# Low parts of layer 1's weights kept in DRAM, and the chunk states as one fp32 product

## The chip, the cores and the metric

The kernel runs on one core of a Trainium2 chip. The metric is the device time of one execution in microseconds, the median of several runs. The engines are named as in the profile: PE (TensorE) multiplies matrices, DVE (VectorE), ACT (ScalarE) and POOL (GpSimd) work on elements, SP (SyncE) issues all DMA transfers here, in order, and each engine works its own queue off in order.

## The reference

One step of a two-layer decoder trunk. Layer 0 mixes tokens by causal pooling, layer 1 by a Mamba-2 scan; 1024 prompt tokens and eight sequences of eight sample tokens pass through the same weights.

```python
def pool_mixer(h, buf, start, w_in, w_mix, scale, w_out):          # layer 0
    uz = h @ w_in
    ...
    y = mixed * scale.astype(jnp.float32) * jax.nn.silu(z.astype(jnp.float32))
    return y.astype(h.dtype) @ w_out, u_ext[:, -POOL_BUF:]

def ssd_scan(x, dt, A, B, C, h0):                                  # in layer 1
    ...
    W = CB[:, :, :, None] * L * dt_t[..., None, :]
    y_diag = jnp.einsum('bcgeij,bcjgep->bcigep', W, x)
    decay_to_end = jnp.exp(a_cum_t[..., -1:] - a_cum_t) * dt_t
    chunk_states = jnp.einsum('bcjgn,bcgej,bcjgep->bcgepn', B, decay_to_end, x)

def ssd_mixer(h, conv_buf, ssm_state, w_in, ...):                  # layer 1
    proj = h @ w_in                  # z, x, B, C and the time steps
    ...                              # convolution, ssd_scan, gate, norm
    return y.astype(h.dtype) @ w_out, new_conv, new_ssm.astype(ssm_state.dtype)
```

The model width is 1024, the inner width 2048; there are four groups of eight heads of 64, a state of 128, and chunks of 128 tokens. All is fp32.

## The kernel before

The tokens go through in two passes h = 0, 1 of 544 columns (512 of the prompt, 32 of the samples), features on the partitions: layer 0 for both passes, then layer 1 for both. The last output products of a layer's pass (`finish`, `pending`) run inside the next pass.

A product is made in fp32r. Each operand is cut into a high part, its fp32r rounding, and a low part, the rest; `product` (L125) adds hi x hi, hi x lo and lo x hi in PSUM, per half of the tokens (272 columns) and per 128 rows of the weight. So a weight unit of 128 x 1024 numbers (512 KB) is 48 matmuls of 272 columns, in two halves for an input unit and four for an output unit. `unit` (L110) loads it into `raw` (two buffers), ACT casts it to `whi` (L119), and DVE or POOL makes `wlo` = `raw` - `whi` (L122; three buffers each). Layer 0 has 112 units. Layer 1 has 57: 40 of `w_sin`, 16 of `w_sout`, and the small `w_dt`; both of its passes make all of them anew, and the last output group loads two a second time. The switch `lowv` gives every L122 to DVE in layer 0 and in the last group, and alternates DVE and POOL otherwise. PSUM has three `big` buffers for products.

In layer 1, a group has six convolved tiles (four of x, then B and C), four gates z and four output units. `ssd_common` (L553) turns B into token-major tiles `bt`, chunk by chunk, through the PSUM tile `tr` (two buffers); `bt` has a high and a low part, and the low part is a DVE subtract (L565) that reads `tr`. `ssd` (L579) goes over the four chunks for a quad of heads: POOL masks the decays `bA`, ACT takes four exponentials (L596), DVE multiplies (L597) and scales x (`xd`, `xs`, L604), and PE makes the diagonal part and the chunk state. For the state `xs` is cut in two by ACT and POOL:

```python
xe = sp.tile([P, 2, 2 * P], F32R, name="xe")
S.copy(xe[:, 0], xs)
G.tensor_tensor(out=xe[:, 1], in0=xs, in1=xe[:, 0], op=ALU.subtract)
for a, (w, k) in enumerate(((0, 0), (0, 1), (1, 0))):
    PE.matmul(pst, bt[:, w], xe[:, k], start=a == 0, stop=a == 2)
```

There are 64 such products (4 groups, 2 quads, 4 chunks, 2 passes).

The order on each engine is set by a scheduler at build time: it takes the instructions in the order of the code, those under `high_priority` (a unit's load, cast and subtract, and the evacuation of products) first, and puts others where its own plan has an engine free.

Of the kernel before, what the change touches and what calls it, by code (L numbers as in the profile page):

```python
# [16 lines left out]
P = 128  # L17
# [25 lines left out]
# columns of the constants array  # L43
# [6 lines left out]
# columns of the parameters array  # L50
# [26 lines left out]
def pool_ssd_step(ctx, tc, xin, spool, sconv, sssm, w_pin, w_mix, w_pout, w_sin, w_dt, w_sout, params, consts,  # L77
# [26 lines left out]
    lowv = [2, 0]  # L104
# [4 lines left out]
    # ---------------------------------------------------------------- helpers  # L109
    def unit(src, cols=1024):  # L110
        raw = wp.tile([P, 1024], F32, name="raw")
        with tc.high_priority():
            return unit1(raw, src, cols)

    def unit1(raw, src, cols):
# [4 lines left out]
        eng = V if lowv[0] and lowv[1] % lowv[0] == 0 else G  # L120
        lowv[1] += 1
        eng.tensor_tensor(out=lo[:, :cols], in0=raw[:, :cols], in1=hi[:, :cols], op=ALU.subtract)  # L122
        return hi, lo

    def product(m, hi, lo, act, kts, width, off, evac, halves=(0, 1)):  # L125
        """evac(n, sum over kt of (hi+lo)[:, kt, off:off+m]^T (ah+al)[kt]) for the halves n of the tokens"""
# [16 lines left out]
    def to_stream(dst, halo, step, r=None):  # L143
        """puts a product (times r) behind the halos of the prompt and of the sample sequences"""
# [39 lines left out]
    def spread(pr, r, quarters):  # L184
        """quarters of r side by side, on every partition"""
# [4 lines left out]
    def rsqrt(ps, count, out=None):  # L190
        """rsqrt(sums / count + eps), on every partition"""
# [30 lines left out]
    def normed(src, r, layer):  # L222
        """hi and lo parts of RMSNorm(x), features on the partitions"""
# [23 lines left out]
    def project(src, act, u, evac):  # L247
        hi, lo = unit(src[u])
# [17 lines left out]
    def out_units(src, g, y, sink):  # L266
        for dpair in range(4):
            out_unit(unit(src[g * 4 + dpair]), dpair, y, sink)

    # ---------------------------------------------------------------- layer 0  # L270
    def layer0(h, act, pending, nxt):
# [48 lines left out]
        def begin():  # L320
            """the first two products, as x comes in; 1 / rms follows them"""
            us = [u_open(m, sp.tile([P, 2 * T], F32, name="ys", bufs=2)[:, :UW]) for m in range(2)]
            lowv[0] = 1
# [36 lines left out]
            lowv[0] = 1  # L360
# [12 lines left out]
        def mix_part(g, p, z):  # L373
            tiles = []
            for mp in range(2):
                hi, lo = unit(w_mix[g * 2 + mp])
                for tt in range(2):
# [51 lines left out]
    # ---------------------------------------------------------------- layer 1  # L429
# [9 lines left out]
    def dt_part(h, act):  # L439
        """time steps and decays; (chunk or sequence, head) on the partitions, their tokens in the columns"""  # L440
        hi, lo = unit(w_dt, KT * NH)
# [18 lines left out]
        # softplus: max(v, 0) + log1p(exp(-|v|)), log1p(e) = 2 artanh(e / (2 + e))  # L460
# [24 lines left out]
        # decay of a whole chunk or sequence, on every partition  # L485
# [7 lines left out]
        # token-major copies  # L493
# [22 lines left out]
    def conv_part(h, act, g, j):  # L516
# [25 lines left out]
        # silu(2 a) = a (1 + tanh a)  # L542
# [10 lines left out]
    def ssd_common(B, C):  # L553
        """per chunk: B with the tokens on the partitions, and the products of B and C"""
        out = []
        for c in range(NCH):
# [432 lines left out]
```

## Time and profile before

| | |
|---|---|
| time, median of 3 runs | 1641.78 us (1641.44 to 1650.25) |
| span of the profiled execution | 1636.0 us, so 5.8 us below the median of the runs |
| PE busy | 1574.1 us (96%) |
| DVE busy | 1173.2 us (72%) |
| ACT busy | 693.1 us (42%) |
| POOL busy | 571.1 us (35%) |
| moved by DMA | 196.75 MB, 120 GB/s on average |

The profile shows one execution; the profiled execution's own time is known as its span, from its first instruction to its last. Layer 0 fills the span up to about 690 us, layer 1 the rest, and its second pass begins at about 1130 us; from about 1590 us on comes the tail, in which the last outputs are normed. Busy shares are means over all of it, so the stages have to be read one by one. A wait is put down to the instruction that ended it.

### The profile page before, as it was taken

What the parts mean: (1) busy time and instruction counts of PE and PEld (TensorE: products, weight loads), DVE (VectorE), ACT (ScalarE), POOL (GpSimd) and SP (SyncE); (2) the same over time, 40 slices, a digit from 0 to 9 for tenths busy, and PEclk for the clock granted to TensorE, in tenths of its full rate; (3) what the DMA queues carried; (4) which work ended last, traced back from release to release, by engine and by line L of the source; (5) the groups of instructions that cost most, each with busy time, mean ns of one, the idle gap of its engine ahead of it and who ended that gap; (6) DMA issues with size and microseconds to landing.
All of it is one profiled execution on the core that took longest, in us unless ns stands there. A gap on an engine that the chain in (4) does not pass through costs nothing. (4 is left out here: it accounts for less than half of the span.)

```text
span 1636.0 us, 32593 instructions
## 1 busy us (share of the span) xinstructions
PE 1574.1 (96%) x12708; PEld 1520.0 (93%) x12708; DVE 1173.2 (72%) x2086; ACT 693.1 (42%) x1405; POOL 571.1 (35%) x657
## 2 busy tenths in 40 slices
PE   9999999999999999989999999999898799899996
PEld 8999999999999999989999999988887799889985
DVE  6566576753646465777885877888869967968877
ACT  5431313333323333455555545544544455435432
POOL 1200000021110010267545455444648546654523
PEclk9999999999999999999999999999999999999998
DMA  5523333345322334336334254344444345353431
GB/s 188 153 91 92 91 99 113 116 134 162 100 87 91 97 99 129 92 114 190 111 126 135 87 150 137 116 132 118 128 130 127 122 126 139 104 148 98 153 118 68
DMA packets 114154, 196.75 MB, mean 120 GB/s; under 512 B 27600, under 2 KB 65616, under 8 KB 114000
## 3 DMA queue, kind: packets, MB, share of 16 engines
q1 hardware_dynamic: 114000, 194.67, 39.5%
q8 instruction: 100, 1.64, 0.4%
q14 instruction: 54, 0.44, 0.1%
HBM read 172.94 MB, written 21.67 MB: 119 GB/s over the span
## 5 line engine op out<-in xcount | busy, mean ns | idle before, releaser
L135 PE MATMUL big<-ah,whi 128*128 128x272 f32 (+1 forms) x2304 | 670.1, 291 | 5.4 <-ACT u L147 5.4
L135 PE MATMUL big<-al,whi 128*128 128x272 f32 (+1 forms) x2304 | 669.1, 290 | 0.0
L135 PE MATMUL big<-ah,wlo 128*128 128x272 f32 (+1 forms) x2304 | 668.7, 290 | 0.0
L135 PEld LDWEIGHTS big<-ah,whi 128*128 128x128 f32 (+1 forms) x2304 | 435.3, 189 | 8.7 <-ACT u L147 5.8
L135 PEld LDWEIGHTS big<-ah,wlo 128*128 128x128 f32 (+1 forms) x2304 | 435.7, 189 | 1.7 <-issue 0.9
L135 PEld LDWEIGHTS big<-al,whi 128*128 128x128 f32 (+1 forms) x2304 | 435.4, 189 | 1.8 <-issue 1.3
L135 PE MATMUL big<-y,whi 128*128 128x272 f32 x2048 | 402.8, 292 | 7.6 <-DVE X L748 6.0
L119 ACT CAST whi<-raw 128x1024 fp32r<-128x1024 f32 (+1 forms) x228 | 237.5, 1041 | 339.2 <-PE big L135 321.6
L135 PEld LDWEIGHTS big<-y,whi 128*128 128x128 f32 x2048 | 323.8, 189 | 14.1 <-DVE X L748 8.0
L122 DVE TENSOR_TENSOR wlo<-raw,whi 128x1024 fp32r<-128x1024 f32 (+1 forms) x171 | 215.4, 1260 | 133.3 <-ACT whi L119 131.3
L135 PE MATMUL big<-y,wlo 128*128 128x272 f32 x1024 | 297.7, 291 | 0.0
L135 PEld LDWEIGHTS big<-y,wlo 128*128 128x128 f32 x1024 | 194.0, 189 | 1.2 <-issue 1.1
L122 POOL TENSOR_TENSOR wlo<-raw,whi 128x1024 fp32r<-128x1024 f32 (+1 forms) x57 | 139.7, 2451 | 99.1 <-ACT whi L119 99.1
L532 DVE SCALAR_TENSOR_TENSOR win<-u,par,win 128x556 f32<-128x556 f32 x144 | 142.6, 990 | 14.1 <-ACT win L530 7.9
L291 POOL COPY uc<-u 128x15 f32<-128x15 f32 x30 | 20.1, 671 | 247.6 <-ACT u L147 167.9
L596 ACT ACTIVATE L<-bA,nat 128x128 f32<-128x128 f32 x256 | 82.3, 392 | 54.8 <-PE dg L607 39.5
L135 PE MATMUL big<-p,whi 128*128 128x272 f32 x512 | 96.4, 288 | 0.0
L389 DVE TENSOR_TENSOR X<-X,big 128x272 f32<-128x272 f32 x128 | 55.0, 432 | 55.2 <-PE big L135 55.2
L698 POOL TENSOR_TENSOR ho<-hs,cdb 128x256 f32<-128x256 f32 x64 | 57.4, 899 | 99.0 <-DMA out_ssm_s_dram<-ho 51.6
L592 POOL TENSOR_SCALAR_AFFINE_SELECT bA<-bA 128x512 f32<-128x512 f32 x64 | 53.4, 835 | 102.7 <-DMA bA<-acd 94.5
L135 PEld LDWEIGHTS big<-p,whi 128*128 128x128 f32 x512 | 80.2, 188 | 0.0
L135 PE MATMUL big<-p,wlo 128*128 128x272 f32 x256 | 73.6, 288 | 0.0
(214 smaller groups left out, 2115.4 us busy)
## 6 DMA issues: line engine op xcount, KB each, us to landing
raw<-in_w_sin_dram SPq DMA_DIRECT2D x80, 512.0 KB, 3.7
raw<-in_w_pin_dram SPq DMA_DIRECT2D x64, 512.0 KB, 3.6
raw<-in_w_sout_dram SPq DMA_DIRECT2D x34, 512.0 KB, 3.6
raw<-in_w_pout_dram SPq DMA_DIRECT2D x32, 512.0 KB, 3.6
bA<-acd SPq DMA_DIRECT2D x64, 256.0 KB, 3.8
hs<-in_sssm_dram SPq DMA_DIRECT2D x64, 128.0 KB, 2.8
raw<-in_w_mix_dram SPq DMA_DIRECT2D x16, 512.0 KB, 3.6
out_ssm_s_dram<-ho SPq DMA_DIRECT2D x64, 128.0 KB, 2.1
```

The source lines that it names most:

```text
L119: S.copy(hi[:, :cols], raw[:, :cols])
L122: eng.tensor_tensor(out=lo[:, :cols], in0=raw[:, :cols], in1=hi[:, :cols], op=ALU.subtract)
L135: PE.matmul(ps, w[:, wsl], x[:, cols], start=first, stop=kt == kts - 1 and a == 2)
L291: G.tensor_copy(out=uc[:, m], in_=u[:, LP:LP + HALO])
L389: return lambda n, ps: V.tensor_tensor(out=half(X[d], n), in0=half(X[d], n), in1=ps, op=ALU.add)
L532: V.scalar_tensor_tensor(out=a[:, :n], in0=x[:, k:k + n], scalar=pcol(V_CW + ti * 4 + k), in1=a[:, :n], op0=ALU.mult, op1=ALU.add)
L592: G.affine_select(out=bA, in_=bA, pattern=[[0, 4], [1, Q]], compare_op=ALU.is_ge, fill=-1e30, base=0, channel_multiplier=-1)
L596: S.activation(out=L[:, e], in_=bA[:, e], func=AF.Exp, bias=nat[:, 0, ci + e:ci + e + 1])
L698: G.tensor_tensor(out=heads(ho), in0=heads(hs), in1=by_head(cdb, (NCH + b) * NH + h0), op=ALU.mult)
```

## The change

Three things are done. `later` and `stash` go through layer 1's weights in 113 pieces, 112 of 512 columns and one of 256: a load into an `L` buffer (three), a cast on ACT into a `bA` buffer (two), a subtract on DVE, and a store into `low`, 57 tensors in DRAM. One piece is asked for with each unit of layer 0, the rest before layer 1. `unit` takes the number of such a tensor: then `wlo` is loaded from it and not computed; without one the subtract is always DVE's. And the chunk state is one fp32 product of `bt` and `xs` without parts, with two buffers for `xs` where there was one.

```diff
+    def stash(n):
+        for k, src, a, b in todo[:n]:
+            raw = sp.tile([P, 512], F32, name="L", bufs=3)[:, :b - a]
+            nc.sync.dma_start(out=raw, in_=src[:, a:b])
+            hl = sp.tile([P, 512], F32R, name="bA", bufs=2)[:, :b - a]
+            S.copy(hl, raw)
+            V.tensor_tensor(out=hl, in0=raw, in1=hl, op=ALU.subtract)
+            nc.sync.dma_start(out=low[k][:, a:b], in_=hl.bitcast(F32))
+        del todo[:n]
...
         S.copy(hi[:, :cols], raw[:, :cols])
-        eng = V if lowv[0] and lowv[1] % lowv[0] == 0 else G
-        lowv[1] += 1
-        eng.tensor_tensor(out=lo[:, :cols], in0=raw[:, :cols], in1=hi[:, :cols], op=ALU.subtract)
+        if k is None:
+            V.tensor_tensor(out=lo[:, :cols], in0=raw[:, :cols], in1=hi[:, :cols], op=ALU.subtract)
+        else:
+            nc.sync.dma_start(out=lo[:, :cols].bitcast(F32), in_=low[k][:, :cols])
         return hi, lo
...
     def project(src, act, u, evac):
-        hi, lo = unit(src[u])
+        hi, lo = unit(src[u], k=LOW_IN + u if src is w_sin else None)
+        stash(1)
         product(P, hi, lo, act, KT, P, 0, evac)
...
-            bt = sp.tile([P, 2, NS], F32R, name="bt", bufs=NCH)
-            S.copy(bt[:, 0], pb[:, 0])
-            V.tensor_tensor(out=bt[:, 1], in0=pb[:, 0], in1=bt[:, 0], op=ALU.subtract)
+            bt = sp.tile([P, NS], F32, name="bt", bufs=NCH)
+            S.copy(bt, pb[:, 0])
...
-            xe = sp.tile([P, 2, 2 * P], F32R, name="xe")
-            S.copy(xe[:, 0], xs)
-            G.tensor_tensor(out=xe[:, 1], in0=xs, in1=xe[:, 0], op=ALU.subtract)
-            for a, (w, k) in enumerate(((0, 0), (0, 1), (1, 0))):
-                PE.matmul(pst, bt[:, w], xe[:, k], start=a == 0, stop=a == 2)
+            PE.matmul(pst, bt, xs, start=True, stop=True)
...
+    later()
     fin, act = layer0(0, None, None, second)
...
     fin, act = layer0(1, act, fin, lambda: normed(x2d[0], rstd[0], 1))
-    lowv[0] = 2
+    stash(len(todo))
     started = head(0, act)
```

The scheduler's order moves with it. On SP in the first pass of layer 0, from the gates of the second pooling group to its next inputs (`raw` is a weight unit, `u` a tile's old tokens), there stood before:

```order
L282 DMA u_1516<-in_spool_dram 128x92
L290 DMA out_pool_s_dram<-u_1060 128x92
L116 DMA raw_1395<-in_w_pin_dram 128x1024
L116 DMA raw_1456<-in_w_pin_dram 128x1024
L116 DMA raw_1519<-in_w_pin_dram 128x1024
L282 DMA u_1594<-in_spool_dram 128x92
L116 DMA raw_1597<-in_w_pin_dram 128x1024
```

In the changed kernel the same place reads so (L133 loads a piece, L137 stores a low part, L146 loads a unit):

```order
L133 DMA L_2633<-in_w_sout_dram 128x512
L316 DMA u_1669<-in_spool_dram 128x92
L146 DMA raw_1603<-in_w_pin_dram 128x1024
L137 DMA low21_107<-bA_2501 128x512
L133 DMA L_2702<-in_w_sout_dram 128x512
L137 DMA low21_107<-bA_2568 128x512
L133 DMA L_2788<-in_w_sout_dram 128x512
L146 DMA raw_1672<-in_w_pin_dram 128x1024
```

Between two units there are now two loads and two stores of pieces. It is so from the third unit of the kernel on to the 58th, almost everywhere; by then all 113 pieces are done.

On DVE in the second pass of layer 1, where the second group begins (L820 scales the first pass's outputs, L719 makes a gate), there stood before:

```order
L820 SCALAR_TENSOR_TENSOR X7_10593<-X7_10593,par_76,rr_15316 128x544
L532 SCALAR_TENSOR_TENSOR win1_16208<-u_16144,par_76,win1_16208 128x556
L597 TENSOR_TENSOR L_15839<-L_15839,bs_15787 128x512
L565 TENSOR_TENSOR bt_15789<-tr_15784,bt_15789 128x128
L719 SCALAR_TENSOR_TENSOR z0_16456<-z0_16456,big_16490 128x272
L597 TENSOR_TENSOR L_15880<-L_15880,bs_15795 128x512
L565 TENSOR_TENSOR bt_15797<-tr_15792,bt_15797 128x128
```

Now (L848 is the old L820, L629 the old L597, L565 the old L532, a step of the convolution):

```order
L848 SCALAR_TENSOR_TENSOR X7_11240<-X7_11240,par_76,rr_15831 128x544
L578 SCALAR_TENSOR_TENSOR p2_16207<-u_16138,win0_16202 128x512
L582 SCALAR_TENSOR_TENSOR p2_16207<-u_16138,win0_16202 128x32
L649 TENSOR_TENSOR ys_16342<-of_16371,bE_16368 128x2x128
L629 TENSOR_TENSOR L_16350<-L_16350,bs_16302 128x512
L629 TENSOR_TENSOR L_16386<-L_16386,bs_16309 128x512
L565 SCALAR_TENSOR_TENSOR win1_16275<-u_16211,par_76,win1_16275 128x556
L629 TENSOR_TENSOR L_16422<-L_16422,bs_16316 128x512
L678 TENSOR_SCALAR Bm_16333<-tr_16331,cst_75 96x128 x4
```

The two subtracts that read `tr` are gone from between the others, and what frees `tr` is a copy on ACT.

On POOL, in the third group of the first pass (L632 decays a state, L592 masks `bA`), there stood before:

```order
L632 TENSOR_TENSOR hf0_11185<-hf0_11145,cdb_7758 128x256
L625 TENSOR_TENSOR xe_11179<-xs_11162,xe_11179 128x256
L592 AFFINE_SELECT bA_11563<-bA_11563 128x512
L625 TENSOR_TENSOR xe_11220<-xs_11203,xe_11220 128x256
L632 TENSOR_TENSOR hf0_11226<-hf0_11185,cdb_7758 128x256
L122 TENSOR_TENSOR wlo_11967<-raw_11964,whi_11966 128x1024
L632 TENSOR_TENSOR hf0_11267<-hf0_11226,cdb_7758 128x256
L625 TENSOR_TENSOR xe_11261<-xs_11244,xe_11261 128x256
```

Now (L660 and L624 are the old L632 and L592):

```order
L660 TENSOR_TENSOR hf0_11818<-hf0_11783,cdb_8493 128x256
L624 AFFINE_SELECT bA_12140<-bA_12140 128x512
L624 AFFINE_SELECT bA_12176<-bA_12176 128x512
L660 TENSOR_TENSOR hf0_11854<-hf0_11818,cdb_8493 128x256
L553 MEMSET u_12902 128x3
L557 COPY u_12902<-cin_8385 128x4x3
L660 TENSOR_TENSOR hf0_11890<-hf0_11854,cdb_8493 128x256
L624 AFFINE_SELECT bA_12212<-bA_12212 128x512
```

The subtracts of `xe` and of the weight unit are gone, and the masks and states follow each other.

## Rows read from the trace of the kernel before

**Rows 1.** Stages: length, busy PE, PEld, DVE, ACT, POOL; clock; DMA share, GB/s.

```profile
0.00:350.00 350.00, 346.44 (x2782) 343.01 (x2782) 224.51 (x401) 121.10 (x176) 26.27 (x54) 1.00 0.38 116
350.00:690.00 340.00, 340.00 (x2718) 338.90 (x2717) 191.60 (x302) 118.82 (x196) 41.12 (x44) 1.00 0.37 110
...
870.00:1050.00 180.00, 176.17 (x1452) 168.79 (x1451) 140.27 (x253) 90.43 (x211) 93.82 (x113) 1.00 0.41 123
...
1230.00:1410.00 180.00, 159.67 (x1244) 153.02 (x1243) 151.09 (x231) 88.88 (x197) 112.76 (x114) 0.95 0.41 124
...
690.00:1590.00 900.00, 856.90 (x6955) 810.25 (x6954) 720.66 (x1315) 442.51 (x1011) 488.59 (x544) 0.99 0.43 128
```

**Rows 2.** PE's waits from 690 us: releaser, us in total, times, longest.

```profile
PE tr L559 <- DVE bt L565: 11.7, 7, 2.7
PE stt L696 <- DVE ho L699: 8.6, 6, 4.3
PE big L135 <- DVE X L748: 6.0, 5, 3.5
PE big L135 <- ACT u L147: 5.4, 2, 2.8
PE tr L168 <- POOL ssq L214: 3.1, 1, 3.1
```

**Rows 3.** Stretches of half clock in layer 1, the longest of five, and their sum.

```profile
1250.20:1257.00 6.80, 5.51 (x24) 5.51 (x25) 6.80 (x6) 3.52 (x7) 6.80 (x8) 0.50 0.37 116
...
sum 20.00, PE 18.34 PEld 18.06 DVE 16.97 ACT 10.03 POOL 10.94; mean PE 3.67 PEld 3.61 DVE 3.39 ACT 2.01 POOL 2.19
```

**Rows 4.** Chain that ended last, in order of time: start, us, matmuls.

```profile
901.44 17.66 PE big L135 x142
...
1621.27 3.73 PE stt L845 x16
```

**Rows 5.** Timeline of PE: the three products of a chunk state, and what follows.

```profile
974.82 0.51 PE L627 MATMUL stt<-xe,bt 128*128 128x256 f32 x3
975.16 0.42 PE L135 MATMUL big<-y,whi 128*128 128x272 f32 x2
```

**Rows 6.** DVE from 690 us by line: busy us, mean ns; idle before.

```profile
L532 DVE SCALAR_TENSOR_TENSOR win<-u,par,win 128x556 f32<-128x556 f32 x141 | 140.2, 994 | 14.1 <-ACT win L530 7.9 <-ACT sat L512 4.2
L122 DVE TENSOR_TENSOR wlo<-raw,whi 128x1024 fp32r<-128x1024 f32 x60 | 79.8, 1331 | 14.4 <-ACT whi L119 12.6 <-POOL cd L507 0.6
L597 DVE TENSOR_TENSOR L<-L,bs 128x512 f32<-128x512 f32 x64 | 61.6, 962 | 5.1 <-ACT bs L562 3.0 <-ACT L L596 2.0
```

**Rows 7.** Two of these lines alone: duration ns min/median/max, first and last start.

```profile
L532 DVE SCALAR_TENSOR_TENSOR win<-u,par,win x141: 775/798/4040, 690.5 to 1523.4; 128x556 f32<-128x556 f32 x141
L597 DVE TENSOR_TENSOR L<-L,bs x64: 669/684/2906, 707.8 to 1554.9; 128x512 f32<-128x512 f32 x64
```

**Rows 8.** Timelines of DVE and of POOL at one moment: start, us.

```profile
1398.46 2.88 DVE L597 TENSOR_TENSOR L<-L,bs 128x512 f32<-128x512 f32 x1
...
1397.87 2.92 POOL L122 TENSOR_TENSOR wlo<-raw,whi 128x1024 fp32r<-128x1024 f32 x1
```

**Rows 9.** POOL from 690 us by line.

```profile
L122 POOL TENSOR_TENSOR wlo<-raw,whi 128x1024 fp32r<-128x1024 f32 (+1 forms) x54 | 132.5, 2454 | 40.0 <-ACT whi L119 40.0
...
L625 POOL TENSOR_TENSOR xe<-xs,xe 128x256 fp32r<-128x256 f32 x64 | 54.5, 851 | 31.2 <-ACT xe L624 31.2
```

**Rows 10.** An ACT cast of 544 columns: duration ns min/median/max.

```profile
L240 ACT CAST p<-sq x32: 630/647/652, 34.6 to 609.5; 128x544 fp32r<-128x544 f32 x32
```

**Rows 11.** DMA issues: count, KB each, median us to landing.

```profile
raw<-in_w_sin_dram SPq DMA_DIRECT2D x80, 512.0 KB, 3.7
...
x2d<-X SPq DMA_DIRECT2D x16, 272.0 KB, 4.1
```

**Rows 12.** Timeline of SP: one issue.

```profile
32.82 0.33 SPq L290 DMA_DIRECT2D out_pool_s_dram<-u  x1
```

**Rows 13.** The stretch of most DMA traffic at the start, columns as in rows 1.

```profile
9.00:12.00 3.00, 2.27 (x26) 1.70 (x27) 2.74 (x3) 3.00 (x5) 1.74 (x2) 1.00 1.03 397
```

More of the change, by code (lines that the diff above doesn't have):

```diff
@@ L103, in pool_ssd_step, with later, inputs, unit @@
     rstd = [None, None]
-    lowv = [2, 0]
     def pcol(i):
         return par[:, i:i + 1]
-    def unit(src, cols=1024):
+    LOW_IN, LOW_OUT, LOW_DT = 0, 40, 56
+    low = [dp.tile([P, 1024], F32, name=f"low{i}") for i in range(57)]
+    todo = []
+    def later():
+        def inputs(g, js):
+            return [16 + (g * 4 + j if j < 4 else 16 + (j - 4) * 4 + g) for j in js]
+        order = [(LOW_DT, w_dt)] + [(LOW_IN + u, w_sin[u]) for u in inputs(0, (4, 5, 0, 1))]
+        for g in range(NG):
+            us = inputs(g, (2, 3)) + [g * 4 + t for t in range(4)]
+            if g + 1 < NG:
+                us += inputs(g + 1, (4, 5, 0, 1))
+            order += [(LOW_IN + u, w_sin[u]) for u in us]
+            order += [(LOW_OUT + g * 4 + d, w_sout[g * 4 + d]) for d in range(4)]
+        for k, src in order:
+            n = KT * NH if k == LOW_DT else 1024
+            for c in range(0, n, 512):
+                todo.append((k, src, c, min(c + 512, n)))
+    def stash(n):
[7 more added lines that the diff above has]
+        del todo[:n]
+    def unit(src, cols=1024, k=None):
         raw = wp.tile([P, 1024], F32, name="raw")
         with tc.high_priority():
-            return unit1(raw, src, cols)
-    def unit1(raw, src, cols):
+            return unit1(raw, src, cols, k)
+    def unit1(raw, src, cols, k=None):
         nc.sync.dma_start(out=raw[:, :cols], in_=src)
@@ L267, in out_units @@
         for dpair in range(4):
-            out_unit(unit(src[g * 4 + dpair]), dpair, y, sink)
+            w = unit(src[g * 4 + dpair], k=LOW_OUT + g * 4 + dpair if src is w_sout else None)
+            stash(1)
+            out_unit(w, dpair, y, sink)
     def layer0(h, act, pending, nxt):
@@ L322, in begin @@
             us = [u_open(m, sp.tile([P, 2 * T], F32, name="ys", bufs=2)[:, :UW]) for m in range(2)]
-            lowv[0] = 1
             pss = [[big.tile([P, 512], F32, name="big") for n in range(2)],
@@ L359, in begin @@
             nc.sync.dma_start(out=cst, in_=consts)
-            lowv[0] = 1
             with tc.high_priority():
@@ L376, in mix_part @@
                 hi, lo = unit(w_mix[g * 2 + mp])
+                stash(1)
                 for tt in range(2):
@@ L439, in dt_part @@
     def dt_part(h, act):
-        hi, lo = unit(w_dt, KT * NH)
+        hi, lo = unit(w_dt, KT * NH, LOW_DT)
         dts = sp.tile([P, 5, TQ], F32, name="dts")
@@ L601, in ssd @@
             xd = sp.tile([P, 2 * P], F32, name="xd", bufs=2)
-            xs = sp.tile([P, 2 * P], F32, name="xs")
+            xs = sp.tile([P, 2 * P], F32, name="xs", bufs=2)
             for k, x1 in enumerate((xd, xs)):
@@ L674, in ssd_sample @@
         xd = sp.tile([P, 2 * P], F32, name="xd", bufs=2)
-        xs = sp.tile([P, 2 * P], F32, name="xs")
+        xs = sp.tile([P, 2 * P], F32, name="xs", bufs=2)
         V.tensor_tensor(out=heads(xd[:SM]), in0=heads(px[:SM]), in1=by_head(sat[:SM, 1], h0), op=ALU.mult)
@@ L869, in finish_last @@
             src = w_sout[(NG - 1) * 4:]
+            lows = LOW_OUT + (NG - 1) * 4
             w = []
-            lowv[0] = 1
             for dpair in range(4):
-                w.append(unit(src[dpair]))
+                w.append(unit(src[dpair], k=lows + dpair))
                 out_unit(w[dpair], dpair, y, add, (0,))
@@ L877, in finish_last @@
             close(0, range(KT))
-            out_unit(unit(src[1]), 1, y, add, (1,))
+            out_unit(unit(src[1], k=lows + 1), 1, y, add, (1,))
             close(1, (6, 7, 4, 5, 0, 1))
             r0 = norm(0, range(KT), False)
-            out_unit(unit(src[0]), 0, y, sink, (1,))
+            out_unit(unit(src[0], k=lows), 0, y, sink, (1,))
             close(1, (2, 3))
@@ L897, in second @@
         return normed(xin[1], rstd[1], 0)
+    later()
     fin, act = layer0(0, None, None, second)
     S.copy(idr, ident)
-    lowv[0] = 1
     fin, act = layer0(1, act, fin, lambda: normed(x2d[0], rstd[0], 1))
-    lowv[0] = 2
+    stash(len(todo))
     started = head(0, act)
```

## The prediction, made before the changed kernel ran

> **What bounds the kernel now.** I read the stages first, then who made TensorE wait, then what the engine it waited for was doing. Columns in the stage table are length, busy time of PE, PE's weight loads, DVE, ACT and POOL, granted clock, DMA share, GB/s. In layer 0 PE is the bound without a break: 340.00 of 340 us busy in the second half, 346.44 of 350 in the first, where the rest is the start [rows 1]. Nothing that relieves another engine there can bring time. In layer 1 up to the tail PE is busy 856.90 of 900 us: 43.1 us are idle [rows 1]. The waits [rows 2] name DVE for most: the transposes of B wait for the subtract L565 that frees their PSUM buffer (11.7 us), state products for the add L699 (8.6), output products for L748 (6.0). Others hang on ACT and POOL (5.4, 3.1). Idleness has a second price: in layer 1 there are five stretches, 20.0 us together, at a granted clock of 0.50, that is 1.2 instead of 2.4 GHz, each just behind such a gap [rows 3]; they cost half their length, 10 us. So some 53 us are to be won in layer 1, and no more.
>
> How idle time follows DVE's load is read in the same table: with DVE busy 140.27 of 180 us (78%) PE idles 3.8 us, with 151.09 (84%) 20.3, with 224.51 of 350 (64%) or 191.60 of 340 only at the start or not at all.
>
> **The change part by part.** The sum is made against the profiled span, 1636.0 us; the median of the runs, 1641.78, is 5.8 us above, and I add the terms to the median.
>
> *The product on PE.* Per chunk three fp32r products of 256 columns become one fp32 product; the starts show 0.34 us from the first of the three to the next matmul [rows 5]. The nearest fp32 row with 128 x 128 weights: eight products of 272 columns, two instructions each, took 3.73 us, 0.466 each, so 0.44 for 256 [rows 4]. That is 0.10 us more, 64 times: **+6 us**, all on the bound engine. Bounds: 0, and +14 if each also loses a slot of a plain matmul (17.66 us / 142 = 0.124 us [rows 4]).
>
> *What leaves DVE and POOL in layer 1.* DVE had 60 weight subtracts there, 79.8 us [rows 6]; the last four units of layer 0's output weights keep theirs, so some 74 us leave, and the 32 subtracts L565 too. POOL loses 132.5 us of weight subtracts and 54.5 us of L625 [rows 9], and ACT the cast before it. With POOL's subtracts something else goes: DVE's L532 has a median of 798 ns and a mean of 994, L597 684 and 962 [rows 6, 7], which over 141 and 64 instructions is 27.6 + 17.8 = 45 us of stretching. A long one stands exactly beside a weight subtract of POOL: L597 for 2.88 us from 1398.46, POOL's from 1397.87 for 2.92 [rows 8]. Other POOL work may stretch them too, and other DVE lines are stretched that I don't count; I take 45. DVE in 690 to 1590 then falls from 720.66 by some 70 (the others lie in the tail) and 45 to about 605 us, 67%.
> The Trainium skill (SBUF — State Buffer, section "SBUF: two separate sides") says that the port which VectorE shares with GpSimd is an exclusive lock held for the whole instruction. The row of 2.88 us agrees. By that rule every stretch beside these two POOL operations would go, in lines not counted here too; that is the third rival's way.
>
> *What that is worth.* At 67% the stages above say less than 3.8 us of idleness per 180; I take 2.8, so 14 us of the 43 stay: **-29 us**. By cause: the waits for L565 become waits for an ACT copy that is there already, L625 is gone, L699 and L748 find a shorter queue; what stays is the start of a pass (time steps, norms), where chains and not loads decide. Bounds: -43, and 0 if each wait finds another last arrival. Of the slow clock's 10 us I take **-7**, as it follows the gaps. In the tail DVE loses a few subtracts of 1.3 us [rows 6], while the last norm's chain stays: **-1** (0 to -4).
>
> *The stash in layer 0.* 112 pieces of 512 columns and one of 256: a load, a cast on ACT, a subtract on DVE, a store. The order does not spread them over layer 0: it puts two into each weight unit for the first 58 units, and none later. A unit is 48 matmuls, 6.0 us at 0.124. A cast is about 0.62 us (0.647 for 544 columns [rows 10]), a subtract 0.68 (as L597's median). DVE gets 113 x 0.68 = 77 us in the first 350, from 64% to 86%; ACT 70, to 55%. What hides it is the depth in front of PE: three weight buffers and three PSUM buffers, two units and two half products ahead. The 86% is the level at which layer 1 loses 20 us in 180, but there the stretches were part of it, and in layer 0 POOL is busy only 26.27 of 350 us [rows 1]. **+4 us**; bounds 0 and +40 (20.3 x 350 / 180, were it like layer 1).
>
> *The loads in layer 1.* Each unit loads its low part, 512 KB more, into a buffer that PE has just left, so SP waits for PE where it waited for the subtract, and the scan's own loads queue behind. A load of that size lands after 3.7 us [rows 11]; the low part is needed two units, 12 us, after its buffer is free. So the weights are hidden with 8 us to spare; the scan's loads may come a little late: **+2 us** (0 to +8).
>
> Sum: +6 - 29 - 7 - 1 + 4 + 2 = -25, so 1611 for the span and **1617 us**.
>
> **The rivals.**
> *The waits change hands.* The gaps stay, with another engine at their end: ACT stands in order behind a weight cast that itself waits for PE, SP behind a low load, and the copies of B or the scan's loads come as late as DVE did. For it: B's chain runs through ACT, and the gaps at the start of a pass are chains. Against: the ordered queue of ACT loses the cast L624 and has 442.51 busy of 900 us [rows 1]. If 33 of 43 us stay and 8 of 10 at the slow clock: +6 - 10 - 2 + 4 + 2 = 0: **1642 us**.
> *The stash's own loop sets layer 0's pace (slower).* It has two buffers and the order ties two pieces to a unit. A buffer comes round after cast 0.62, subtract 0.68, issue 0.33 [rows 12], and the store's landing: 4.1 us for 272 KB [rows 11], 5.7 together, against a unit's 6.0. The next unit's weight cast stands behind it in ACT's queue. If landing takes 5.1 us in the crowd, a unit takes 6.7 and 58 units lose 41 us less the 12 us of lead: +29, which against -29 elsewhere is even; at 5.4 it is 1.0 us a unit, +46, and **1659 us**. So it decides from a mean landing of 5.1 us. For it: loads and stores come to 262 GB/s from weights and pieces, about 290 with the rest of the first stage's traffic. Against: the queue moved 397 GB/s in 9 to 12 us [rows 13], and ACT, at 55%, has 2.7 us of a unit free before the next weight cast.
> The Trainium skill (DMA: Bandwidth & Descriptors, section "Specifications") gives about 358 GB/s as one core's share of HBM; the row of 397 GB/s stands above it, and by either the traffic fits, so it does not raise this chance.
> *Nearly all idleness goes.* DVE relieved of more stretching than counted, 4 us stay, 1 at the slow clock: +6 - 39 - 9 - 2 + 0 + 0 = -44: **1598 us**.
> *It does not do what it says:* low parts land after PE wants them. Excluded by the 8 us above but for a jam of the queue; 2 in 100, counted as slower.
>
> **How the numbers follow.** Forecast 1606 to 1631: 0.46. Nearly all goes, 1593 to 1606: 0.20. Waits change hands, 1631 to 1650: 0.19. The loop, over 1650: 0.13, and the last 0.02. The range 1598 to 1649 leaves out the better half of the third rival's cases (0.06 to 0.1) and the slower ones (0.12). Half a per cent, 8 us, is about what a measurement tells from no change: below 1633.6 faster, 0.66; to 1650 same, 0.19; above, slower, 0.15.
>
> **What would show it.** Right: in layer 1 PE idles 10 to 20 us in the 900, no wait for the B subtract or L625 is left, the medians and means of L532 and L597 fall together, DVE is near 67%, the state product shows two instructions of about 0.22 us apart, at most two stretches at 0.50 clock remain; layer 0 still shows no gap over a microsecond behind the start, and DVE some 86% in its first half. Wrong: gaps in the first 350 us behind ACT casts that wait for a store (the loop), or gaps in layer 1 of the old size that end with ACT or a DMA (changed hands).

## The result, and the profile after

The changed kernel takes **1614.78 us** (median of four runs, 1614.12 to 1620.24), the kernel before 1641.61 in the same comparison; the ratio is 0.984, with a 95% interval of 0.982 to 0.986. The profiled span fell from 1636.0 to 1612.3 us. The forecast was 1617 us, faster. So the size is right. The reason, as the runs below show, is so only in part.

I read the stages first. Columns as in [rows 1]: the stretch, its length, busy time of PE, PE's weight loads, DVE, ACT and POOL, clock, DMA share, GB/s. Kernel after:

```profile
0.00:350.00 350.00, 338.76 (x2689) 333.60 (x2690) 282.57 (x499) 179.30 (x276) 28.25 (x50) 0.99 0.85 276
350.00:690.00 340.00, 340.00 (x2718) 338.90 (x2717) 187.92 (x296) 119.24 (x194) 30.33 (x40) 1.00 0.41 122
690.00:1570.00 880.00, 865.05 (x6992) 818.01 (x6991) 586.51 (x1254) 433.12 (x965) 253.36 (x430) 0.99 0.62 197
690.00:1590.00 900.00, 883.36 (x7168) 835.86 (x7168) 602.21 (x1284) 437.38 (x972) 266.33 (x445) 0.99 0.61 195
```

In layer 1 PE idles 880 - 865.05 = 15.0 us, where 43.1 of 900 stood before [rows 1]; DVE is at 67%. In the first 350 us PE has 2689 matmuls behind it, before it was 2782: 93 fewer, at 0.124 us [rows 4] 11.6 us. The second half of layer 0 is as gapless as it was. So layer 1 gave and layer 0 took.

What PE waits for in layer 1 (releaser, us in total, times, longest), kernel after:

```profile
PE big L166 <- DVE X L776: 3.5, 3, 2.5
PE big L166 <- DVE z L747: 3.3, 2, 2.8
PE tr L219 <- DVE dts L212: 2.4, 2, 1.6
PE stt L724 <- DVE ho L727: 2.3, 3, 1.2
...
PE tr L592 <- ACT bt L597: 0.5, 1, 0.5
```

Against [rows 2]: the 11.7 us for the second part of `bt` became 0.5 us for ACT's copy; the 8.6 us for `ho` (then L699, now L727) became 2.3, the 6.0 for X (then L748, now L776) 3.5. What is left are mostly chains at the start of a pass (`dts`, X, z).

Stretches at half the clock (0.50 is 1.2 of 2.4 GHz), kernel after, the first in layer 0, two in layer 1:

```profile
87.00:93.80 6.80, 4.99 (x27) 4.51 (x28) 6.77 (x18) 3.45 (x5) 1.13 (x4) 0.50 0.75 248
1087.10:1093.90 6.80, 6.03 (x28) 5.45 (x29) 6.80 (x14) 3.76 (x9) 0.61 (x1) 0.50 0.41 131
1230.40:1233.80 3.40, 3.40 (x17) 3.40 (x16) 3.40 (x4) 0.00 (x0) 3.15 (x3) 0.51 0.99 314
```

Layer 1 has 10.2 us of them, before 20.0 [rows 3]. Each stands again behind a gap of PE: 2.8 us that end at 1087.9, 2.5 at 1230.0, and in layer 0 4.9 at 87.4.

That gap in layer 0, on the timelines of PE and then of ACT (start, us; in brackets the idle time ahead and who ended it):

```profile
82.25 0.28 PE L166 MATMUL big<-ah,wlo 128*128 128x272 f32 x1
87.42 0.68 PE L199 MATMUL tr<-ssq,ones 128*32 128x136 f32 x8 [4.89 <-POOL ssq L245]
...
80.80 0.63 ACT L135 CAST bA<-L 128x512 fp32r<-128x512 f32 x1
81.33 1.05 ACT L149 CAST whi<-raw 128x1024 fp32r<-128x1024 f32 x1
85.23 0.66 ACT L244 ACTIVATE sq<-sq 128x544 f32<-128x544 f32 x1 [2.86 <-DMA sq<-in_xin_dram]
```

PE wants the column sums of the second pass's x. The load of the last tile of x stands on SP between the loads and stores of the pieces; it goes out at 80.35 and lands at 85.1. Then come ACT's square, POOL's add, and PE. The chain of waits of the same stretch shows the pieces themselves (start, us, what):

```profile
42.83 6.41 DMA low<-bA
56.25 4.86 DMA low<-bA
62.55 4.42 DMA low<-bA
67.72 4.31 DMA low<-bA
73.50 5.21 DMA low<-bA
80.35 4.78 DMA sq<-in_xin_dram
```

Last, the operations the prediction spoke of. DVE's two stretched lines in layer 1 (busy us, mean ns | idle before):

```profile
L565 DVE SCALAR_TENSOR_TENSOR win<-u,par,win 128x556 f32<-128x556 f32 x144 | 118.4, 823 | 46.6 <-ACT win L563 43.9
L629 DVE TENSOR_TENSOR L<-L,bs 128x512 f32<-128x512 f32 x64 | 50.2, 796 | 8.7 <-ACT L L628 4.9 <-ACT bs L595 3.7
```

The means were 994 and 962 ns [rows 6]: they fell together. And the state product (duration ns min/median/max, first and last start):

```profile
L655 PE MATMUL stt<-xs,bt x128: 377/379/483, 728.5 to 1546.7; 128*128 128x256 f32 x128
```

It is two instructions, 128 for 64 products.

### The profile page after: what moved, and what is told of

Same layout as the page of the kernel before. It is cut to its first block, busy times and chain, and to the rows that moved or that the text cites. A ratio compares the mean times of both kernels' runs of the same rounds, so it can differ in the third digit from the quotient of the medians.

```text
span 1612.3 us, 33214 instructions
## 1 busy us (share of the span) xinstructions
PE 1571.3 (97%) x12644; PEld 1515.7 (94%) x12644; DVE 1086.4 (67%) x2108; ACT 740.6 (46%) x1454; POOL 325.7 (20%) x536
## 4 chain that ended last, share of the span: by engine, by line
PE 81%; DMA 8%; DVE 5%; ACT 2%; issue 2%; POOL 1%; SPq 0%; DVEq 0%; ACTq 0%; POOLq 0%
PE big L166 70%; DMA low<-bA 4%; PE dg L639 2%; PE stt L655 2%; PE of L648 2%; DMA bA<-acd 1%; DMA bAs<-asd 1%; PE tr L632 1%; DMA sq<-x2d 1%; DVE bA L136 1%; DMA L<-in_w_sin_dram 1%; PE big L386 1%; PE stt L724 1%; PE of L720 1%; DVE wlo L151 1%
## 5 line engine op out<-in xcount | busy, mean ns | idle before, releaser
L151 DVE TENSOR_TENSOR wlo<-raw,whi 128x1024 fp32r<-128x1024 f32 x112 | 139.2, 1243 | 107.6 <-ACT whi L149 105.7
L565 DVE SCALAR_TENSOR_TENSOR win<-u,par,win 128x556 f32<-128x556 f32 x144 | 118.4, 823 | 46.6 <-ACT win L563 43.9
L135 ACT CAST bA<-L 128x512 fp32r<-128x512 f32 (+1 forms) x113 | 69.9, 619 | 95.4 <-DMA low<-bA 80.0
L136 DVE TENSOR_TENSOR bA<-L,bA 128x512 fp32r<-128x512 f32 (+1 forms) x113 | 78.9, 701 | 32.9 <-ACT bA L135 32.7
L624 POOL TENSOR_SCALAR_AFFINE_SELECT bA<-bA 128x512 f32<-128x512 f32 x64 | 48.5, 759 | 162.6 <-DMA bA<-acd 136.0
L726 POOL TENSOR_TENSOR ho<-hs,cdb 128x256 f32<-128x256 f32 x64 | 49.4, 778 | 138.4 <-DMA out_ssm_s_dram<-ho 79.5
L178 ACT COPY u<-big 128x272 f32<-128x272 f32 (+2 forms) x192 | 52.6, 308 | 50.9 <-PE big L166 34.4
```

Source lines behind the costliest of these rows:

```text
L135: S.copy(hl, raw)
L136: V.tensor_tensor(out=hl, in0=raw, in1=hl, op=ALU.subtract)
L151: V.tensor_tensor(out=lo[:, :cols], in0=raw[:, :cols], in1=hi[:, :cols], op=ALU.subtract)
L178: S.copy(out, ps)
L565: V.scalar_tensor_tensor(out=a[:, :n], in0=x[:, k:k + n], scalar=pcol(V_CW + ti * 4 + k), in1=a[:, :n], op0=ALU.mult, op1=ALU.add)
L624: G.affine_select(out=bA, in_=bA, pattern=[[0, 4], [1, Q]], compare_op=ALU.is_ge, fill=-1e30, base=0, channel_multiplier=-1)
```

## The experiments

All times are medians; "layer 0" is when the first step of the scan's convolution (the line that reads `win<-u,par,win`) starts, "layer 1" the time from its first start to its last, in the profiled execution; the last two columns are DVE's busy time and PE's idle time in 690 to 1590 us (in the faster kernels a little of the tail is in it).

| kernel | us | ratio to before (95%) | layer 0 | layer 1 | DVE | PE idle |
|---|---|---|---|---|---|---|
| before | 1641.6 | | 683.0 | 840.4 | 720.66 | 43.1 |
| after | 1614.8 | 0.984 (0.982 to 0.986) | 693.5 | 810.6 | 602.21 | 16.6 |
| product alone | 1634.7 | 0.996 (0.994 to 0.997) | 683.0 | 842.9 | 703.77 | 36.3 |
| low parts from DRAM alone | 1625.6 | 0.989 (0.987 to 0.992) | 696.9 | 818.4 | 602.22 | 26.2 |
| all subtracts on DVE | 1625.9 | 0.989 (0.984 to 0.994) | 683.3 | 827.9 | 721.85 | 34.0 |
| after, POOL's load put back | 1640.6 | 0.999 (0.997 to 1.001) | 695.9 | 831.0 | 622.42 | 29.4 |
| after, no pieces | 1597.8 | 0.973 (0.971 to 0.975) | 681.6 | 803.7 | 603.40 | 22.9 |
| after, pieces spread | 1605.3 | 0.977 (0.975 to 0.980) | 690.6 | 803.2 | 604.03 | 14.2 |
| all subtracts on DVE, and product | 1602.4 | 0.975 (0.974 to 0.977) | 681.9 | 810.0 | 719.64 | 16.5 |
| that, and the squares' adds on DVE | 1596.3 | 0.973 (0.971 to 0.975) | 683.4 | 802.2 | 739.97 | 19.8 |

The kernel without pieces and the last one reach the tail earlier; from 690 to 1570 us they idle 14.8 and 14.0 us, as the changed kernel does with 15.0.

**The two halves apart.** The product alone, on the kernel before:

```diff
-            bt = sp.tile([P, 2, NS], F32R, name="bt", bufs=NCH)
-            S.copy(bt[:, 0], pb[:, 0])
-            V.tensor_tensor(out=bt[:, 1], in0=pb[:, 0], in1=bt[:, 0], op=ALU.subtract)
+            bt = sp.tile([P, NS], F32, name="bt", bufs=NCH)
+            S.copy(bt, pb[:, 0])
...
+            PE.matmul(pst, bt, xs, start=True, stop=True)
```

> The kernel before with the state product of the change alone: one plain fp32 product of the chunk's B and x, no second part of B, no cast and no POOL subtract of x; the weights' low parts are still made in layer 1, on VectorE and GpSimd in turn. My theory, that the gain is VectorE's queue getting shorter and no longer stretched beside the weight subtracts, leaves 60 weight subtracts and most of the stretching here: the waits for the B subtract (11.7 us) go, the product costs 64 x 0.08 = 5 us more, some 6 us of other idleness goes with GpSimd's subtract of x: about 1629 us, L532 at a mean of 900 to 1000 ns still. The rival, that the waits for B's subtract and the product's three parts were the cause, gives the whole gain without layer 0's stash: 1641.6 - 26.8 - 11.7, about 1603. A second rival, that the waits change hands, gives 1642 to 1647 (the product's 5 us and nothing back).

And the changed kernel with these lines as they were before:

> The changed kernel with the state product of the kernel before (three fp32r products, B's second part by a VectorE subtract out of PSUM, x's by GpSimd); the low parts still come from DRAM. My theory gives most of the gain to this half: layer 0 11.7 us longer as in the changed kernel, layer 1 with 5 us less of PE for the products and some 10 us of idleness more than the changed kernel (B's subtract), so 1614.8 + 5 = about 1620; L532's mean near 850 ns. If the product's half were the cause: 1641.6 + 11.7 = 1653. If the two halves only add up, this one and the product alone together give -26.8.

They gave -7 and -16 us, together -23 of the -27. The rival that the waits for B's subtract were the cause falls (1603 expected, 1634.7 measured). Both ended between 5 and 6 us above what I expected.

**Load or stretching.** In the kernel before, all of layer 1's weight subtracts go to DVE:

```diff
-    lowv[0] = 2
+    lowv[0] = 1
     started = head(0, act)
```

> The kernel before with all weight subtracts of layer 1 on VectorE and none on GpSimd (in before they take turns). It sets VectorE's load against the stretching. VectorE gets some 54 subtracts of 1.24 us more (+67 us on the 720 of 690 to 1590 us) and, by the theory that GpSimd's weight subtracts stretched L532 and L597, loses up to 45 us of stretching: about 745 us, 83%, so the idleness of layer 1 stays near 43 us: about 1641. If the load alone decides and nothing is stretched less: 88% and some 20 us more, 1660. If the stretching (or GpSimd's 2.9 us subtract in the chain of a unit) alone decides: 43 down to 20 us, 1615 to 1620. The means of L532 and L597 say which: 994 and 962 ns, or 820 and 790.

1625.9 us. The stage row of this kernel:

```profile
690.00:1590.00 900.00, 866.02 (x7050) 823.16 (x7049) 721.85 (x1382) 444.26 (x1015) 376.05 (x488) 0.98 0.44 129
```

DVE's lines in 690 to 1570 us:

```profile
L122 DVE TENSOR_TENSOR wlo<-raw,whi 128x1024 fp32r<-128x1024 f32 x110 | 145.5, 1323 | 22.0 <-ACT whi L119 19.5 <-PE dg L607 0.9
L532 DVE SCALAR_TENSOR_TENSOR win<-u,par,win 128x556 f32<-128x556 f32 x141 | 122.1, 866 | 3.5 <-ACT win L530 0.6 <-POOL cc L527 0.5 <-POOL bA L592 0.3
L597 DVE TENSOR_TENSOR L<-L,bs 128x512 f32<-128x512 f32 x64 | 50.0, 781 | 1.2 <-ACT L L596 1.2
```

And PE's largest wait in 690 to 1590 us:

```profile
PE big L135 <- ACT u L147: 12.9, 3, 8.9
```

DVE does 113 weight subtracts in 690 to 1590 us where it did 57, 150.4 us against 76.0, and its busy time is 721.85 us against 720.66. What 56 subtracts add, the lines that are less stretched give back: 18.1 us in L532, 11.6 in L597, and 29.6 in four lines that the forecast did not count (L244, L549, L665, L753). With the same load PE idles 9 us less, and 8.9 us of the rest is a single wait.

The opposite edit: the changed kernel, with POOL's subtracts back, off the path:

```diff
             nc.sync.dma_start(out=lo[:, :cols].bitcast(F32), in_=low[k][:, :cols])
+            turn[0] += 1
+            if turn[0] % 2 == 0:
+                for a in range(0, cols, 512):
+                    b = min(a + 512, cols)
+                    G.tensor_tensor(out=dump[:, :b - a], in0=raw[:, a:b], in1=hi[:, a:b], op=ALU.subtract)
```

> The changed kernel with GpSimd's load put back off the path: in every second unit of layer 1 GpSimd subtracts the weights' high part from the weights as in the kernel before, in two pieces of 512 columns, into a tile that nobody reads. The low parts still come from DRAM. By the theory that these subtracts stretch VectorE, L565's mean goes from 823 back towards 990 ns and L629's from 796 to 960, VectorE gets up to 45 us more in layer 1 (67 to 72%), and the idleness of 15 us grows by 4 to 12: 1619 to 1627. By the rival that only VectorE's own subtracts and the chain through them counted: 1614.8, the means unchanged. Buffers of weights come free later by GpSimd's reading of them, which may cost a little in either case.

1640.6 us: the whole gain is gone, and the loss is more than twice what I expected. The stage row:

```profile
690.00:1590.00 900.00, 870.61 (x6989) 820.48 (x6988) 622.42 (x1254) 428.30 (x964) 408.63 (x538) 0.99 0.61 192
```

The lines of POOL's subtract and of DVE's two in 690 to 1570 us:

```profile
L161 POOL TENSOR_TENSOR dump<-raw,whi 128x512 f32<-128x512 f32 x106 | 150.0, 1415 | 38.8 <-ACT whi L152 37.6
L573 DVE SCALAR_TENSOR_TENSOR win<-u,par,win 128x556 f32<-128x556 f32 x144 | 134.8, 936 | 41.2 <-ACT win L571 36.6 <-ACT sat L553 2.1
L637 DVE TENSOR_TENSOR L<-L,bs 128x512 f32<-128x512 f32 x64 | 52.4, 827 | 9.9 <-ACT L L636 5.1 <-ACT bs L603 4.4
```

And one moment on the timelines of DVE and of POOL:

```profile
1407.99 2.68 DVE L573 SCALAR_TENSOR_TENSOR win<-u,par,win 128x556 f32<-128x556 f32 x2
...
1408.79 1.28 POOL L161 TENSOR_TENSOR dump<-raw,whi 128x512 f32<-128x512 f32 x1
```

Nobody reads `dump`. At 1408 two steps of the convolution, 1.6 us at their median of 798 ns, take 2.68 us, with POOL's subtract of 1.28 us beside the second. L573's mean went back from 823 to 936 ns, but L637's only from 796 to 827, where I had expected 960. DVE is at 69%, far below the kernel before, and PE idles 29.4 us. Layer 1 is 20.4 us longer than in the changed kernel; about 12.8 of it are idleness, 3.4 the half clock (17.0 us in five stretches, against 10.2 in two), and the rest is open.

So POOL's subtracts cost 26 us, but the run doesn't show that they cost it by stretching alone. Only some gaps of PE stand right behind a stretched instruction (1.0 us up to 1005.8, 2.2 up to 1252.7). Four others, 7.8 us together (up to 793.4, 897.3, 1203.4 and 1368.5), stand behind a DVE that sat idle in its order for the load of `bAs`, and three, 4.8 us, end with POOL's own work. The waits of DVE and of SP in 690 to 1590 us, and then one such gap on the timelines of DVE and PE:

```profile
DVE bAs L701 <- DMA bAs<-asd: 56.5, 16, 7.5
SPq L149 <- POOL dump L161: 144.7, 45, 7.0
...
1202.27 0.78 DVE L701 TENSOR_SCALAR bAs<-bAs,sat 32x32 f32<-32x32 f32 x4 [5.42 <-DMA bAs<-asd]
1203.44 0.52 PE L174 MATMUL big<-y,whi 128*128 128x272 f32 x2 [2.89 <-DVE z L755]
```

In the changed kernel DVE waits 29.0 us for `bAs`. SP issues that load in its order, and here it stands 144.7 us for POOL to free a weight buffer. So the later release of these buffers is a rival that this run leaves in part. Against it: no wait of PE in layer 1 ends with a weight's cast or load (the largest is for `ho` on DVE, 8.8 us), and in the next kernel SP stands 131.8 us for DVE's subtracts to free them while PE idles 16.5. Nor is the added work the only difference, as the scheduler places everything anew with each edit: of layer 1's instructions on DVE and on ACT more than a tenth stand in another order than in the changed kernel. The other pairs of kernels were not compared in this, and the same may be so there.

Then both kinds of POOL subtracts away, with nothing made in layer 0: the product alone, and `lowv[0] = 1`.

> The kernel before with the new state product and all weight subtracts of layer 1 on VectorE: GpSimd is free of weight subtracts and of x's, and nothing is made in layer 0. It tells how much of the gain is GpSimd's work going and how much VectorE's load. If the halves add up: the product alone gave -7, the subtracts on VectorE -16, so 1641.7 - 23 = 1619. By the theory formed after the runs so far, that VectorE's stretched instructions and not its load make PE wait, this comes close to the changed kernel freed of its layer-0 cost (the paced one, 1605): 1606 to 1612. If VectorE's load still counts (some 78% here against 67%), 1615 to 1622.

1602.4 us, 12 us faster than the changed kernel, without its DRAM tensors. Its stage row:

```profile
690.00:1590.00 900.00, 883.48 (x7148) 835.18 (x7147) 719.64 (x1386) 436.00 (x968) 337.94 (x440) 0.99 0.43 129
```

Its lines on DVE in 690 to 1570 us:

```profile
L122 DVE TENSOR_TENSOR wlo<-raw,whi 128x1024 fp32r<-128x1024 f32 x113 | 144.5, 1279 | 28.4 <-ACT whi L119 26.8 <-DMA bA<-acd 0.5
L532 DVE SCALAR_TENSOR_TENSOR win<-u,par,win 128x556 f32<-128x556 f32 x140 | 115.6, 826 | 3.4 <-POOL cout L526 0.9 <-ACT win L530 0.4
```

This row beside that of before is the study in one line: DVE 719.64 and 720.66 us busy, PE idle 16.5 and 43.1. And beside that of after: DVE 719.64 and 602.21, PE idle 16.5 and 16.6; layer 1 810.0 and 810.6 us long. That each half alone gave so little (-7 and -16 against -39 together) is not explained in full: each leaves one kind of POOL subtract (54.5 or 132.5 us, [rows 9]). One part is seen in DVE's waits in 690 to 1590 us. It stood idle for POOL's `xe` (L625 of the kernel before) for 31.6 us in the kernel before, 51.5 with the low parts from DRAM alone and 26.3 with all subtracts on DVE; with the new product this wait is gone. `xs` has two buffers then where it had one, which no run tries by itself.

Further in the same direction: the 58 adds of squares go from POOL to DVE.

```diff
-                G.tensor_tensor(out=acc, in0=acc, in1=sq, op=ALU.add)
+                V.tensor_tensor(out=acc, in0=acc, in1=sq, op=ALU.add)
...
-                G.tensor_tensor(out=ssq[0], in0=ssq[0], in1=sq, op=ALU.add)
+                V.tensor_tensor(out=ssq[0], in0=ssq[0], in1=sq, op=ALU.add)
```

> The kernel of the product and all weight subtracts on VectorE (1602.4 us, nothing made in layer 0), with GpSimd's 58 adds of squares (1.5 us each, two of them at the end of the chain to a norm) on VectorE as well. By the theory that long GpSimd instructions stretch VectorE's and that VectorE's load does not make PE wait at this level, VectorE's busy time grows by less than 58 x 0.7 = 41 us, the gap that ended with GpSimd's add (4.4 us and the half clock behind it) shrinks: 1594 to 1600. If VectorE's load counts above 78%: 1605 to 1615.

1596.3 us, the lowest median here: 44 us under the kernel before in its own comparison, and 18 under the changed one. It is 6 under the kernel of 1602.4, but the two intervals overlap. To see whether DVE's load has a price higher up, the kernel of 1602.4 us gets the three products again, with all their parts made by ACT and DVE:

> The same kernel of 1602.4 us with three fp32r products for the chunk state, whose parts ScalarE and VectorE make from SBUF, off the path and without GpSimd. PE saves 64 x 0.08 = 5 us and VectorE gets some 30 us more, to about 82%. On the paced kernel the same edit gave -3.8 (1605.3 to 1601.5). If VectorE's load does not count: 1597 to 1599. If it does at 82%: 1603 to 1612.

The edit in short: `bt` and `xe` have two parts again, `S.copy(bc, pb[:, 0])` takes B out of PSUM once, and `V.tensor_tensor` makes the low parts. 1609.0 us (0.981, 0.979 to 0.984), 6.6 more and not 4 less; DVE is at 84% (760.37 us), the mean of L532 back at 887 ns, PE idles 24.8 us. That DVE's load is the reason isn't shown: the product's chain is longer, ACT has more to do, and PE's largest wait is for ACT's copy of `u` (10.2 us, of which 7.4 in one gap). The same edit on the changed kernel with its pieces spread:

> The changed kernel with the pieces spread over layer 0 as in the paced one, and with three fp32r products for the chunk state again, but off the path: ScalarE copies B out of PSUM once, and both parts of B and of x are made from SBUF by ScalarE and VectorE, none by GpSimd. PE saves 64 x 0.08 = 5 us; VectorE gets 64 subtracts of 256 columns and 32 of 128, some 30 us, 67 to 70%, and ScalarE the casts. Against the paced kernel's 1605.3: 1600 if VectorE's load costs nothing as long as it is not stretched; 1605 to 1610 if the longer chain to the product makes PE wait.

1601.5 us (0.976, 0.974 to 0.978) against 1605.3 (0.977, 0.975 to 0.980): the intervals overlap, and the profiled execution was slower (1606.9 against 1603.6), so its 5 us on PE are not shown.

**What the pieces cost in layer 0.** The changed kernel with 2 of the 113 pieces:

```diff
-    low = [dp.tile([P, 1024], F32, name=f"low{i}") for i in range(57)]
+    low = [dp.tile([P, 1024], F32, name="low")] * 57
...
-        for k, src in order:
+        for k, src in order[1:2]:
```

> The changed kernel without the stash: only one weight tensor's low part is made in layer 0 (2 pieces of 113), and every unit of layer 1 loads that one; so layer 1's products use wrong low parts, and nothing else is left out. It prices the 111 other pieces. The trace after shows layer 0 11.7 us behind the kernel before; if that is all due to the pieces, this gives 1614.8 - 11.7 = 1603. My prediction's +4 would give 1611. Layer 1 should be unchanged, its matmuls at the same distances from its first.

1597.8 us. Every unit of layer 1 then loads the one low part that is made. Layer 0 gets 11.9 us back (693.5 to 681.6), as expected. Layer 1 is 7 us shorter too, which I had not expected; the gap of 2.8 us up to 1087.9 and the half clock behind it, which the changed kernel has, are not in this one. In the changed kernel DVE stands 4.5 us there for a load of x2d; why that load comes in time here is open.

Pieces spread over all of layer 0, by one ring for a piece's load and result:

```diff
-            raw = sp.tile([P, 512], F32, name="L", bufs=3)[:, :b - a]
+            raw = sp.tile([P, 512], F32, name="bA", bufs=2)[:, :b - a]
```

> The changed kernel with the pieces spread: the load's tile comes from the same two-buffer ring as the result, so the order has one piece in each weight unit over all of layer 0 in place of two in each of the first 58. Of the theory that the 11.7 us are a jam (x loads of the second pass behind stash traffic on the queue, casts that wait for landings, at the two-per-unit rate), most goes: layer 0 within 3 us of the kernel before, 1614.8 - 9 = 1606. Of the rival that each piece costs its own (113 pieces x 0.1 us), wherever it stands: 1614.8. Of the rival that VectorE's 64 to 86% is what costs (not the queue): DVE comes to about 75% in both halves, the gap at 82 us shrinks by half: 1609.

1605.3 us, the time that the theory of the jam gave (1606), but not for its reason: layer 0 gave 2.9 us back where I expected 9 and stays 7.6 above the kernel before. The rest came from layer 1 (803.2 us, as without pieces), of which the theory said nothing. Stage rows of layer 0:

```profile
0.00:350.00 350.00, 344.64 (x2760) 340.31 (x2761) 254.12 (x453) 151.96 (x229) 28.54 (x53) 1.00 0.64 198
350.00:690.00 340.00, 336.85 (x2683) 334.71 (x2682) 217.43 (x348) 146.64 (x244) 41.32 (x39) 1.00 0.65 203
```

And its stores (count, KB each, median us from issue to landing):

```profile
low<-bA SPq DMA_DIRECT2D x112, 256.0 KB, 3.1
```

The gap at 82 us is gone; small ones for DVE (1.2 to 1.7 us each) stand in either half, so spread pieces still cost.

Two kernels were to tell DVE's load from the stores. Without the pieces' subtract:

> The changed kernel whose pieces are loaded, cast and stored, but not subtracted: what is stored is the high part, so layer 1's low products are wrong. VectorE is then free of 79 us in layer 0's first stretch. The order packs the pieces closer without it, two to three in a unit. If VectorE's load (64 to 86%) is what costs layer 0 its 11.7 us, they go: 1603. If the casts that wait for the stores' landing in ScalarE's queue (77 us of such waits in the first 350 us) and the queue are what costs, they stay or grow: 1614 to 1622.

Without the pieces' stores, but for one tensor:

> The changed kernel whose pieces are loaded, cast and subtracted, but stored for one weight tensor only, which every unit of layer 1 then loads, so layer 1's low products are wrong. The casts no longer wait for a store to land before they may write the buffer again. The order packs the pieces closer, three to a unit, so VectorE is loaded as much, in a shorter time. By the theory that the casts' waits for stores in ScalarE's queue cost layer 0 its 11.7 us: 1603 to 1606. If VectorE's load costs them: 1614 or more, with PE waiting for VectorE in the first 250 us.

1628.3 (0.991, 0.988 to 0.994) and 1613.2 us (0.982, 0.977 to 0.987). Of the kernel without the subtract, the stage row, and then ACT's largest wait in the first 350 us:

```profile
0.00:350.00 350.00, 331.17 (x2578) 324.53 (x2579) 210.45 (x380) 175.42 (x272) 26.40 (x49) 0.98 0.85 278
```

```profile
ACT bA L135 <- DMA low<-bA: 117.5, 87, 3.5
```

Of the kernel without the stores, the stage row, and then PE's largest wait in the first 350 us:

```profile
0.00:350.00 350.00, 334.91 (x2653) 328.95 (x2654) 284.51 (x501) 180.49 (x276) 29.68 (x49) 1.00 0.63 198
```

```profile
PE big L167 <- DVE X L423: 6.0, 6, 2.0
```

With DVE at 60%, less than before the change [rows 1], the first loses more than the changed kernel (layer 0 to 707.3 us), and its casts wait 117.5 us for stores. The second has no stores to wait for and loses as well (698.0 us), now with DVE at 81% and PE waiting for it. Since the order packed the pieces closer in both (two to three, and three to a unit), neither cause is shown to be the only one; what goes with the loss in all four is how many pieces stand in a unit: one 690.6, two 693.5, about three 698.0 and 707.3.

## Why the prediction was right, and where not

By parts, on the profiled spans: layer 0 was 10.5 us longer (forecast +4, the stash); layer 1, first to last step of the convolution, 29.8 us shorter (forecast -28: product, idleness, half clock and low loads, +6 - 29 - 7 + 2); from there to the end 4.4 us shorter (forecast -1). The sum is -23.7, forecast -25. That it is so near is in part luck: layer 0 lost 6.5 us more than forecast, the end and layer 1 gave 5.2 more.

- **The product, +6.** Right: where it stands alone between plain matmuls, the starts show 0.43 to 0.44 us for it and 0.36 for the three: 0.08 x 64 = +5.
- **The idleness of layer 1, -29.** Right in size (43.1 to 15.0 us, forecast 14), wrong in its reason. The step that failed is the one that read idleness from DVE's load. In [rows 1] the stages with a low DVE share are also those with a low POOL share (26.27 of 350 and 41.12 of 340 us in layer 0, 93.82 and 112.76 of 180 in layer 1); I took the first for the cause, and had the second under stretching, as 45 us of load. The run with DVE's load as before and POOL's subtracts gone has PE idle 16.5 us, and the run with DVE at 69% and POOL's subtracts back 29.4. So what POOL does makes PE wait, not the sum of DVE's work, up to about 82%. At 84% PE idled more again, in a kernel whose product also hangs on a longer chain. One way in which POOL does it stands on the timelines of DVE, POOL and PE of the kernel before, at its longest gap:

```profile
1243.19 3.34 DVE L752 SCALAR_TENSOR_TENSOR p<-p,par,ys 128x544 f32<-128x544 f32 x2
1246.46 4.65 DVE L753 SCALAR_TENSOR_TENSOR p<-p,z 128x544 f32<-128x544 f32 x2
1242.79 4.95 POOL L817 TENSOR_TENSOR X<-X,sq 128x544 f32<-128x544 f32 x3
1247.70 2.82 POOL L122 TENSOR_TENSOR wlo<-raw,whi 128x1024 fp32r<-128x1024 f32 x1
1251.49 0.58 PE L696 MATMUL stt<-xh,Bm 96*128 96x256 f32 x1 [4.34 <-DVE ho L699]
```

Four DVE instructions, 2.97 us by their medians (771 and 714 ns), take 7.99 us beside POOL's adds and weight subtract, and the `ho` that PE wants stands behind them. The other ways are waits in order, for `xe` and for loads that came late. How the idleness divides between them is not shown.

- **The stretching, 45 us.** It was mis-sized. I counted it in two lines; DVE took 56 more weight subtracts, 74 us, at the same busy time, and the product's POOL subtract was still there. The rival that named this (nearly all idleness goes, 1598 us) was right that more is stretched than I counted, but not in what follows: 15.0 us of idleness stayed, as I had forecast, and not 4. The convolution's means were 823 ns in the changed kernel, 936 with POOL's subtracts back and 826 in the kernel of 1602.4 us, which has neither kind; at 1408 two steps took 2.68 us. The Trainium skill (SBUF — State Buffer, section "SBUF: two separate sides") calls the port that VectorE and GpSimd share an exclusive lock, held for the whole instruction. These numbers agree with that.
- **The half clock, -7.** Its price in layer 1 fell from 10 to 5.1 us: -5, and layer 0 got 3.4 that I had not counted.
- **The stash, +4.** The mis-sized term: 10.5 us at the start of layer 1. My sign for layer 0, no gap over a microsecond behind the start, did not hold. I had sized DVE at 86% (measured 282.57 of 350, 81%) and took the depth of buffers as cover. The cover holds for the weights, whose waits are small (0.6 us for `wlo` and 0.5 for `whi`, both at the very start). It doesn't hold for the x tiles of the second pass: their loads stand on SP between pieces, and I named nothing behind the pieces on that queue but weights. This gap is not all of the cost: with the pieces spread it is gone, and 7.6 us stay. The rival of the loop was there in small: ACT's casts wait 72 times for a store, 77.2 us in all, and the chain of waits runs through stores of 4.3 to 6.4 us. Their median of 4.0 is below its point of 5.1, and the pace of a unit held but for 12 us.
- **The low loads in layer 1, +2.** No wait of PE for a low part was seen; 512 KB land in 3.7 us, as its row had it. The scan's loads did come later: `bAs` landed after a median of 4.4 us where it had been 2.5, and DVE waited 29.0 us for it where it had been 17.1. And the loads bought little: layer 1 with the subtracts on DVE is as long (810.0 us against 810.6; 803.2 with the pieces spread).

The rivals: the waits did not change hands (0.5 us for ACT's copy of B), and no low part came after PE wanted it. But DRAM isn't what makes the kernel fast. Of the change, the part that pays is what POOL no longer does; the stash costs 10.5 us for that, where DVE could have taken the work at the same length of layer 1.

## What to carry to other kernels

Before work is taken off an engine, look at the mean and the median of its instructions: where the mean is far above, ask what disturbs it before what loads it. Here it paid to still the disturber even by giving the disturbed engine more to do. When a table of stages is to show what idleness follows, look which other column rises with it. And work that is put under the cover of a busy engine's stage stands in the queues of all others: go through what is queued behind each of its transfers, the rare ones too.

## What the runs showed of the hardware

- POOL's subtract of 512 columns (1.4 us) in every second weight unit, whose result nobody read, cost 26 us of 1615, with DVE at 69% and POOL at 45% of the time; how much of it by stretched DVE instructions and how much by later loads is not shown.
- DVE's busy time in 900 us did not change by 2 us when it took 56 weight subtracts (74 us) from POOL.
- A store of 256 KB landed after a median of 4.0 us with the queue at 276 GB/s, and after 3.1 us at 198 to 203 GB/s.
